# Modulation of a two-layer diffusion trunk: its products between the large ones in bursts of eight row blocks instead of four

## The chip, the cores and the metric

One core of a Trainium2 chip runs the whole program. The metric is device time in microseconds (us) of one execution, the median of several. TensorE multiplies, VectorE and ScalarE do the elementwise work, GpSimd a little of it, and SyncE issues nearly all DMA transfers, in one queue.

## The reference

One inference step of a trunk of two layers, for 128 context tokens and 128 latent tokens with the same weights, all in float32. For each layer:

```
mod = SiLU(cond) @ w_mod[l] + b_mod[l]      # cond: 2 vectors of 2048; w_mod[l]: 2048 x 12288
sh1, sc1, g1, sh2, sc2, g2 = split(mod, 6)
h   = rmsnorm(x) * (1 + sc1) + sh1
mix = mixers(h @ w_in)                      # latent attention | 2-D Fourier | RWKV-7 scan
x   = x + g1 * rmsnorm(mix @ w_out)
h   = rmsnorm(x) * (1 + sc2) + sh2
u   = dwconv3(h @ w_up) + b;  gate, val = split(u, 2)
x   = x + g2 * rmsnorm((silu(gate) * val) @ w_down)
```

The modulation is a product of two rows with 100 MB of weights per layer. Its first part is needed before the first product of a layer, its last part at the end.

## The kernel before

**Large products.** The 256 tokens (both groups side by side) are the moving operand, 128x128 pieces of a weight are the stationary one. To keep float32 accuracy each operand is split in two float32r halves: `hi` is the rounded value, `lo` the rest. `mm3` (lines 335 to 339) multiplies hi by hi, hi by lo and lo by hi: three products on TensorE for each piece. For the weights `weights_` (line 312) loads a tile of 128x2x512 into one of the 7 buffers of the pool `raw` (512 KB), ScalarE writes `hi` (L327), VectorE writes `lo` (L328). Pools of 3 hold the hi and the lo. A weight's instructions are traced 60 places ahead of their turn (`WP`), so that it is loaded and split early. For the input h of a sub-layer `pre_norm` (line 465) makes, for each of four groups of 512 features, eight pieces `h` on VectorE (L485), eight `hh` on ScalarE (L486) and eight `hl` on VectorE (L487).

**Modulation.** `modulation` (line 232) makes 512 of the 12288 columns. The stationary operand is a 128x32 piece of the silu of the two conditions (2 of 32 columns are used), the moving one a row block of 128 rows by 512 columns of w_mod. The 16 row blocks are spread over four strips of 32 columns of the array (q), so that four products can run at the same time; each strip sums every fourth block in its own 32 partitions of the PSUM tile `mb`. Then VectorE transposes `mb` to `pm` (L245), TensorE adds up the four strips (`mc`, L249), VectorE adds the bias (`mod`, L254) and makes scale factors of it (`modx`, L288 and L290). Being float32, each of these products stands as two records in the trace.

**How it is spread.** `modulation` is a generator. A step (`mod_step`, line 258) is one advance of it: four row blocks (two loads of 512 KB with two row blocks each, then the four products), or the transpose. 48 such generators stand in a queue in a fixed order. `gemm` and `gemm_k` call `tick` after each half tile of weights; `tick` (line 275) adds a rate, set by hand for each stage (`MR`, `AR`, `QR`, `FR`), to a credit, and makes a step for each full credit. `need` makes steps until a given group is done; `pre_norm` and the last parts of each sub-layer call it. Before the first layer's mixers (`early`) the modulation's rows lie in the pool of slabs (20 buffers), later in the pool `raw`, which they share with the weights.

**Order.** The program is traced by one Python process; a scheduler then orders each engine's instructions by priority (the place at which they were traced, moved by `WP` for the weights) and by when it reckons that their inputs and buffers are there. On the chip every engine and SyncE's queue go through their list in that order.

Of the kernel before, what the change touches and what calls it, by code (L numbers as in the profile page):

```python
# [38 lines left out]
NV, NV2 = sum(r for _, r in VEC), sum(r for _, r in VEC2)  # L39


# buffers of each pool; columns of the modulation made before the first layer; pieces that GpSimd takes; order of the pieces
RAW, HI, SLAB, HALF = 7, 3, 20, 22
BMM = 3
SV = 4
# [1 line left out]
POOLX = (5, 6)  # L47
ORD = (0, 1, 5, 2, 3, 6, 4, 7)
YG = ((0, 1), (5,), (2, 3), (6,), (4,), (7,))
# how the steps of the scan and of the modulation are spread over the products, by layer and phase  # L50
RA = [
    [[0.8, 0.8, 0.8], [0.8, 1.16, 0.96], [0.56, 0.8, 0.8], [0.8], [0.95, 0.95, 0.95, 0.95], [0.95, 1.0, 0.8, 1.0], [1.0, 1.0, 1.3]],
    [[0.8, 0.8, 0.578], [0.88, 0.8, 0.8], [0.96, 0.8, 0.8], [1.0], [1.0, 1.0, 1.0, 1.0], [1.287, 1.3, 1.183, 1.3], [1.45, 1.45, 1.45]],
# [15 lines left out]


class Lazy:
    """the items of a generator, traced as they are asked for"""

    def __init__(self, gen):
        self.gen, self.items = gen, []
# [7 lines left out]
class Trunk:  # L83
# [47 lines left out]
        o = VOFF[name] + k0  # L131
        return (self.vec2 if name.startswith("ffn") else self.vec[l])[:, o:o + n]

    # ---------------------------------------------------------------- set-up
    def setup(self):
        nc, i = self.nc, self.i
        self.const = self.cp.tile([128, C_LATER], F32, name="const")
        nc.sync.dma_start(self.const, i["const"][:, 0:C_LATER])
        self.later = self.cp.tile([128, C_N - C_LATER], F32, name="later")
        self.ident = self.c(C_ID, 128)  # L140
        self.eps = self.cp.tile([128, 2], F32, name="eps")
        nc.vector.memset(self.eps[:, 0:1], EPS)
        nc.vector.memset(self.eps[:, 1:2], GN_EPS)
        self.zero = self.cp.tile([128, 64], F32, name="zero")
        nc.vector.memset(self.zero, 0.0)
        self.seg = self.cp.tile([128, 256], F32, name="seg")
        nc.vector.memset(self.seg, 1.0)
        nc.vector.memset(self.seg.rearrange("p (s t) -> p s t", t=128)[:, :, 0:1], 0.0)
        self.vec = [self.cp.tile([128, NV], F32, name=f"vec{l}") for l in range(L)]
        self.mod = [self.cp.tile([128, 96, 2], F32, name=f"mod{l}") for l in range(L)]  # L150
        self.modx = [self.cp.tile([128, 4, 16, 2], F32, name=f"modx{l}") for l in range(L)]

        cr = self.small([32, 128], "vr", bufs=1)
        nc.sync.dma_start(cr[0:16], i["c_ctx"].rearrange("(k p) -> k p", p=128))
        nc.sync.dma_start(cr[16:32], i["c"].rearrange("o (k p) -> (o k) p", p=128))
        self.cst = self.cp.tile([128, 16, 32], F32, name="cst")
        nc.vector.memset(self.cst, 0.0)
        b = self.bank([128, 2, 16])
        nc.tensor.transpose(b.rearrange("p g k -> p (g k)"), cr, self.ident[0:32, 0:32])
        nc.scalar.activation(self.cst[:, :, 0:2], b.rearrange("p g k -> p k g"), AF.Silu)  # L160

        self.new_x()
        for g, nm in enumerate(("x_prompt", "x_sample")):
            for k in range(4):
                if k % 2 == 0:
                    r = self.raw([128, 8, 128])
                    nc.sync.dma_start(r, i[nm][0, :, 512 * k:512 * k + 1024].rearrange("t (k p) -> t k p", p=128))
                b = self.bank([128, 4, 128])
                for j in range(4):
                    nc.tensor.transpose(b[:, j, :], r[:, 4 * (k % 2) + j, :], self.ident)  # L170
                for e in range(2):
                    nc.vector.tensor_copy(self.x[2 * k + e][:, :, 128 * g:128 * g + 128], b[:, 2 * e:2 * e + 2, :])

        for _ in range(SV):
            self.mod_step()
        self.finish(self.load_vec(0, VEC, self.vec[0]))

    def new_x(self):
# [51 lines left out]
        return r  # L230

    def modulation(self, l, i):
        """512 columns of the modulation on the tensor engine: every fourth chunk of the rows in a strip of 32 columns"""
        nc = self.nc
        w = self.i["w_mod"][l]
        b = self.pmod.tile([128, 512], F32, tag="m", name=self.name("mb"))
        for kg in range(4):
            for e in range(2):
                r = self.mod_raw(w, i, 512 * kg + 256 * e)
                for f in range(2):  # L240
                    q = 2 * e + f
                    nc.tensor.matmul(b[32 * q:32 * q + 32, :], self.cst[:, 4 * kg + q, :], r[:, f, :], start=kg == 0, stop=kg == 3)  # L242
            yield
        m = self.half([128, 4, 4, 32], nm="pm")
        nc.vector.transpose(m.rearrange("p j a c -> p (j a c)"), b)  # L245
        yield
        b2 = self.pmod.tile([128, 4, 2], F32, tag="m", name=self.name("mc"))
        for a in range(4):
            nc.tensor.matmul(b2[32 * a:32 * a + 32], self.c(C_SEL, 32), m[:, :, a, 0:2], start=True, stop=True)  # L249
        self.mod_end(l, i, b2)  # L250
# [7 lines left out]
    def mod_step(self):  # L258
        while True:
            if self.modgen is None:  # L260
                if not self.modq:
                    return False
                self.modgen = self.modulation(*self.modq[0])
            try:
                next(self.modgen)
                return True
            except StopIteration:
                self.modgen = None
                self.done.add(self.modq.pop(0))
# [5 lines left out]
    def tick(self, n=1.0):  # L275
        self.credit += self.rate * n
        while self.credit >= 1:
            self.credit -= 1
            self.mod_step()

    def mod_scale(self, l, which, k):
        nc = self.nc
# [6 lines left out]
        else:  # L289
            nc.vector.tensor_tensor(out, src, g, op=ALU.mult)  # L290

    # ---------------------------------------------------------------- pieces
    def split(self, src, nm):
        nc = self.nc
        hi = self.slab(list(src.shape), F32R, nm + "h")
# [70 lines left out]
                    self.tick(0.5)  # L366

    def gemm_k(self, wsrc, cols, rhs, evac, rates):
        """like gemm, one group of 512 input features after the other, with all the sums open at once"""
        banks = []  # L370
        for c0, w in cols:
            banks.append([(self.mm_bank if n < BMM else self.bank)([128, 2, 256])
# [47 lines left out]
            nc.tensor.matmul(ps, self.c(C_ONE, 128), sq[:, j, :], start=first and j == 0, stop=last and j == n - 1)  # L420

    def sumsq4(self, ps, src, c0):
        """like sumsq over 16 chunks, with the sums of every fourth chunk in a strip of 32 columns"""
        nc = self.nc
        n = src.shape[1]
        sq = self.half([128, n, 256], nm="sq")
        nc.scalar.activation(sq, src, AF.Square)
        for j in range(n):
            c = c0 + j
            q = 32 * (c % 4)  # L430
            nc.tensor.matmul(ps[q:q + 32, :], self.c(C_ONE, 32), sq[:, j, :], start=c < 4, stop=c >= 12)  # L431
# [7 lines left out]
        return out  # L439

    def rsqrt(self, out, src, scale, eps, tmp):
        """out = 1 / sqrt(scale * src + eps): the table's value, then a Newton step"""
        nc = self.nc
        v, t = tmp
        nc.scalar.activation(out, src, AF.Abs_reciprocal_sqrt, bias=self.eps[:, eps:eps + 1], scale=scale)
        nc.scalar.activation(v, src, AF.Identity, bias=self.eps[:, eps:eps + 1], scale=scale)
        nc.vector.scalar_tensor_tensor(t, out, -0.5, out, op0=ALU.mult, op1=ALU.mult)
        nc.vector.tensor_tensor(t, t, v, op=ALU.mult)
        nc.vector.scalar_tensor_tensor(out, t, 1.5, out, op0=ALU.add, op1=ALU.mult)  # L449
# [5 lines left out]
        return rs  # L455

    def arm(self, after):
        """brings in the table that the next norm needs, once after is there"""
        t = self.small([128, 2], "arm", bufs=1)
        self.nc.scalar.activation(t, after, AF.Abs_reciprocal_sqrt, bias=self.c(C_ONE, 1), scale=0.0)  # L460

# [1 line left out]
        return rs.unsqueeze(1).to_broadcast([128, n, 256])  # L463

    def pre_norm(self, l, which):
        """a generator: the normed and modulated input, split, by groups of 512 features"""
        nc = self.nc
        sh0 = (0, 48)[which]
        a = self.modx[l][:, 2 * which]
# [43 lines left out]
            nc.vector.scalar_tensor_tensor(uv[:, :, 1:128], pv[:, :, 0:127], w0, uv[:, :, 1:128], op0=ALU.mult, op1=ALU.add)  # L513
            nc.vector.scalar_tensor_tensor(uv[:, :, 0:127], pv[:, :, 1:128], w2, uv[:, :, 0:127], op0=ALU.mult, op1=ALU.add)  # L514

    # ---------------------------------------------------------------- mixers
    def in_proj(self, l, h, st, names, outer=False):
        nc = self.nc
        cols = {"kv": (512, 320), "q": (0, 512), "xf": (832, 512), "r": (1344, 512), "k": (1856, 512), "v": (2368, 512), "lo": (2880, 256)}
# [187 lines left out]
    def rwkv_scan(self, l, st):  # L707
# [16 lines left out]
        U = {}  # L724

        def pre(z):
            """normalised key, token-major values (as they are and reversed) of two channel chunks"""
            kh = self.half([128, 2, 256], nm="kh")
            tt(kh, st["k", z], b2(vec("rwkv_k_k", 2 * z, 2), 256), op=ALU.mult)
            wa = self.half([128, 2, 256], nm="wa")  # L730
# [204 lines left out]
    def rwkv_solve(self, l, st, z):  # L935
# [6 lines left out]
        C = st["C"][z]  # L942
        AP, RH, bon, lo = C["AP"], C["RH"], C["bon"], st["lo"]
        y, v = st["rw", z], st["v", z]
        # inverses of the 32 x 32 blocks on the diagonal
        G = self.slab([128, 32, 32], nm="G")
        nc.gpsimd.memset(G[:, :, 16:32], 0.0)
        for d in range(2):
# [18 lines left out]
                yield INV * IW  # L967
        XT = M
        nc.vector.transpose(XT.rearrange("p n t -> p t n"), X)
        # solve block by block; the right-hand side turns into the solution  # L970
        for j in range(4):
            js = slice(32 * j, 32 * j + 32)
            for d in range(2):
# [26 lines left out]
                           start=d == 0 and e == 0 and g == 0, stop=d == 1 and g == 1 and e == 1)  # L1000
        tt(y, y, ya.rearrange("p e g t -> p e (g t)"), op=ALU.add)
        yield YW
        # group norm, bonus, gate
        sv = self.half([128, 2, 256], nm="sq")
        g2 = self.half([128, 256], nm="g2")
        nc.sync.dma_start(g2, i["rwkv_g2"][l][:, 256 * z:256 * z + 256])
# [51 lines left out]
            nc.gpsimd.dma_start(o["state"][0, l, d, 4 * z:4 * z + 4].rearrange("h v k -> v h k"), so.rearrange("v (h k) -> v h k", k=64))  # L1058
            yield TW

    # ---------------------------------------------------------------- layer
    def merge(self, a, b, na, nb):
        """a's steps with b's spread over them"""
        credit = 0.0
        for _ in a:
            credit += nb / na
# [205 lines left out]
```

## Time and profile before

| | |
|---|---|
| time, median of 3 runs | 2782.31 us (2780.23 to 2782.39) |
| profiled execution, first to last instruction | 2799.7 us |
| instructions | 53893 |
| TensorE busy | 2701.2 us, 96% |
| VectorE, ScalarE, GpSimd busy | 61%, 43%, 4% |
| moved by DMA | 594 MB, 212 GB/s on average |
| granted clock of TensorE, mean | 0.979 |

The profile is one execution, not one of the three timed ones; the page gives no other time of it than its span. Stages of the span, roughly: up to 165 us set-up and the first layer's first in_proj (k, r, v and the low-rank columns); to 600 us its mixers with the rest of in_proj and the output projection; to 1490 us its gated MLP; to 2020 us the second layer's in_proj and mixers; then the second layer's MLP. The modulation is spread from 13 to 1890 us.

In a row of the timeline the columns are start, duration, engine, line, operation, output and inputs, shapes and count; in brackets stands the idle time ahead of it and what ended that. In a table of windows: stretch, its length, busy time of TensorE with the number of its records, granted clock (1.00 is 2.4 GHz, 0.50 is 1.2), busy share of the DMA engines and GB/s.

### The profile page before, as it was taken

The numbers are of one execution on the slowest core, as the hardware profiler recorded it, in microseconds if no ns is written. First come the engines' busy times: TensorE is split into PE (matmuls) and PEld (weight loads), VectorE is DVE, ScalarE is ACT, GpSimd is POOL, SyncE is SP. The second block draws the span as 40 slices with busy tenths as digits, with TensorE's granted clock in tenths as the row PEclk, the third lists the DMA queues.
The fourth block names the chain that finished last, engine by engine and source line by source line (L and its number), as shares of the span: only waits on it lengthen the run. The fifth ranks groups of instructions, "written<-read, shape, count | busy, mean of one in ns | idle before, by whom it ended". The sixth has DMA issues, their size and how long they took to land. (4 is left out here: it accounts for less than half of the span.)

```text
span 2799.7 us, 53893 instructions
## 1 busy us (share of the span) xinstructions
PE 2701.2 (96%) x22531; PEld 2383.4 (85%) x22531; DVE 1695.1 (61%) x2690; ACT 1208.4 (43%) x1747; POOL 124.8 (4%) x130
## 2 busy tenths in 40 slices
PE   7999999989999999999998999999799999999997
PEld 4577778758888988888886987878699999999997
DVE  3377848576564465545556688685766546654665
ACT  2256424344343344334444466353454434443453
POOL 1111000010000000000000020000100000000000
PEclk9999989999999999999999999998899999999998
DMA  9965636778777877788776654443355555555552
GB/s 364 372 208 179 204 102 209 239 249 273 262 260 266 273 265 264 263 268 271 250 256 203 215 184 152 162 141 132 97 181 181 184 185 181 182 183 186 181 181 84
DMA packets 316501, 594.46 MB, mean 212 GB/s; under 512 B 22758, under 2 KB 38146, under 8 KB 316256
## 3 DMA queue, kind: packets, MB, share of 16 engines
q1 hardware_dynamic: 314624, 589.54, 63.5%
q8 instruction: 177, 2.90, 0.4%
q0 software_dynamic: 1632, 1.46, 0.2%
q14 instruction: 68, 0.56, 0.1%
HBM read 583.78 MB, written 7.14 MB: 211 GB/s over the span
## 5 line engine op out<-in xcount | busy, mean ns | idle before, releaser
L328 DVE TENSOR_TENSOR lo<-raw,hi 128x1024 fp32r<-128x1024 f32 (+1 forms) x712 | 854.8, 1204 | 756.0 <-ACT hi L327 716.1
L327 ACT CAST hi<-raw 128x1024 fp32r<-128x1024 f32 (+1 forms) x712 | 733.0, 1030 | 1035.1 <-PE mm L338 839.0
L337 PE MATMUL mm<-hh,hi 128*128 128x256 f32 x3360 | 958.9, 288 | 9.6 <-ACT hh L486 8.7
L338 PE MATMUL mm<-hl,hi 128*128 128x256 f32 x3360 | 953.1, 284 | 1.5 <-DVE hl L487 0.8
L339 PE MATMUL mm<-hh,lo 128*128 128x256 f32 x3360 | 950.7, 284 | 0.9 <-DVE lo L328 0.9
L337 PEld LDWEIGHTS mm<-hh,hi 128*128 128x128 f32 x3360 | 644.4, 192 | 79.4 <-issue 57.9
L338 PEld LDWEIGHTS mm<-hl,hi 128*128 128x128 f32 x3360 | 646.5, 192 | 10.1 <-issue 6.0
L339 PEld LDWEIGHTS mm<-hh,lo 128*128 128x128 f32 x3360 | 645.9, 192 | 5.7 <-issue 3.5
L337 PE MATMUL mm<-gh,hi 128*128 128x256 f32 x1408 | 401.2, 286 | 0.0
L339 PE MATMUL mm<-gh,lo 128*128 128x256 f32 x1408 | 398.8, 283 | 0.0
L338 PE MATMUL mm<-gl,hi 128*128 128x256 f32 x1408 | 398.5, 283 | 0.0
L337 PEld LDWEIGHTS mm<-gh,hi 128*128 128x128 f32 x1408 | 269.6, 192 | 22.8 <-issue 22.6
L339 PEld LDWEIGHTS mm<-gh,lo 128*128 128x128 f32 x1408 | 269.9, 192 | 4.1 <-issue 4.1
L338 PEld LDWEIGHTS mm<-gl,hi 128*128 128x128 f32 x1408 | 270.0, 192 | 3.3 <-issue 3.3
L242 PE MATMUL mb<-raw,cst 128*32 128x512 f32 x1536 | 256.3, 612 | 8.3 <-DMA raw<-in_w_mod 4.3
L510 ACT ACTIVATE u<-mm,vec 128x256 f32<-128x256 f32 x176 | 94.6, 562 | 115.8 <-DVE u L514 84.1
L337 PE MATMUL mm<-mxh,hi 128*128 128x256 f32 x384 | 117.2, 307 | 0.3 <-ACT hi L327 0.3
L338 PE MATMUL mm<-mxl,hi 128*128 128x256 f32 x384 | 112.3, 293 | 0.3 <-DVE mxl L298 0.3
L339 PE MATMUL mm<-mxh,lo 128*128 128x256 f32 x384 | 111.5, 292 | 0.6 <-DVE lo L328 0.6
L513 DVE SCALAR_TENSOR_TENSOR u<-mm,vec,u 128x254 f32<-128x254 f32 x176 | 80.1, 475 | 32.7 <-ACT u L510 32.7
L337 PEld LDWEIGHTS mm<-mxh,hi 128*128 128x128 f32 x384 | 75.3, 197 | 21.0 <-issue 16.6
L496 POOL TENSOR_TENSOR d<-d,rs 128x512 f32<-128x512 f32 x8 | 13.4, 1694 | 1713.0 <-DVE rs L449 1713.0
(344 smaller groups left out, 3130.0 us busy)
## 6 DMA issues: line engine op xcount, KB each, us to landing
raw<-in_w_mod SPq DMA_DIRECT2D x384, 512.0 KB, 5.5
raw<-in_ffn_w_up SPq DMA_DIRECT2D x352, 512.0 KB, 4.5
raw<-in_ffn_w_down SPq DMA_DIRECT2D x176, 512.0 KB, 4.7
raw<-in_w_in SPq DMA_DIRECT2D x80, 512.0 KB, 5.2
raw<-in_w_out SPq DMA_DIRECT2D x64, 512.0 KB, 5.4
raw<-in_w_uq SPq DMA_DIRECT2D x16, 384.0 KB, 4.9
raw<-in_w_in SPq DMA_DIRECT2D x16, 320.0 KB, 3.3
raw<-in_w_in SPq DMA_DIRECT2D x16, 256.0 KB, 3.7
```

What stands on the lines that cost most here:

```text
L242: nc.tensor.matmul(b[32 * q:32 * q + 32, :], self.cst[:, 4 * kg + q, :], r[:, f, :], start=kg == 0, stop=kg == 3)
L327: nc.scalar.copy(hi[:, :, 0:w], r)
L328: nc.vector.tensor_tensor(lo[:, :, 0:w], r, hi[:, :, 0:w], op=ALU.subtract)
L337: mm(out, whi, xhi, start=start, stop=False)
L338: mm(out, whi, xlo, start=False, stop=False)
L339: mm(out, wlo, xhi, start=False, stop=stop)
L496: e.tensor_tensor(d, d, self.bc(rs, 2), op=ALU.mult)
L510: nc.scalar.activation(u[:, m, :], ps[:, m, :], AF.Identity, scale=w1, **kw)
L513: nc.vector.scalar_tensor_tensor(uv[:, :, 1:128], pv[:, :, 0:127], w0, uv[:, :, 1:128], op0=ALU.mult, op1=ALU.add)
```

## The change

A burst takes eight row blocks: `modulation` now asks for four loads at once (four tiles of 512 KB) and then traces eight products, two for each strip, before it yields. `mod_step` returns how many of the old steps that was (2 for a burst, 1 for the transpose), and `tick` takes it from the credit, so that the average rate is as before. Lines behind the change move by one, and comments are gone; both are left out here.

```
-        for _ in range(SV):
-            self.mod_step()
+        n = 0
+        while n < SV:
+            n += self.mod_step()
...
-        for kg in range(4):
-            for e in range(2):
-                r = self.mod_raw(w, i, 512 * kg + 256 * e)
-                for f in range(2):
-                    q = 2 * e + f
-                    nc.tensor.matmul(b[32 * q:32 * q + 32, :], self.cst[:, 4 * kg + q, :], r[:, f, :], start=kg == 0, stop=kg == 3)
-            yield
+        for k2 in range(0, 4, 2):
+            rs = [self.mod_raw(w, i, 512 * k2 + 256 * e) for e in range(4)]
+            for kg in (k2, k2 + 1):
+                for q in range(4):
+                    r = rs[2 * (kg - k2) + q // 2]
+                    nc.tensor.matmul(b[32 * q:32 * q + 32, :], self.cst[:, 4 * kg + q, :], r[:, q % 2, :], start=kg == 0, stop=kg == 3)
+            yield 2
         m = self.half([128, 4, 4, 32], nm="pm")
         nc.vector.transpose(m.rearrange("p j a c -> p (j a c)"), b)
-        yield
+        yield 1
...
                 if not self.modq:
-                    return False
+                    return 1
                 self.modgen = self.modulation(*self.modq[0])
             try:
-                next(self.modgen)
-                return True
+                return next(self.modgen)
...
         while self.credit >= 1:
-            self.credit -= 1
-            self.mod_step()
+            self.credit -= self.mod_step()
```

Three places show what this does to the order. Names: `mb` is the sum of one modulation group, `raw` a loaded tile, `gh` and `gl` the halves of the MLP's inner values, `hi` and `lo` those of a weight; a number counts tiles and differs between the two programs.

On TensorE, in the first layer's MLP (its first down-projection), before: two bursts of four, 48 large products apart.

```order
4919 L339 MATMUL mm_8970<-gh_8695,lo_9172 128x256
4920 L242 MATMUL mb_9100<-raw_9205,cst 32x512 x2
4921 L242 MATMUL mb_9100<-raw_9209,cst 32x512 x2
4922 L337 MATMUL mm_8969<-gh_8695,hi_9177 128x256
...
4969 L339 MATMUL mm_9242<-gh_6964,lo_9246 128x256
4970 L242 MATMUL mb_9100<-raw_9279,cst 32x512 x2
4971 L242 MATMUL mb_9100<-raw_9283,cst 32x512 x2
4972 L337 MATMUL mm_9241<-gh_6964,hi_9251 128x256
```

The same place now:

```order
4919 L338 MATMUL mm_8972<-gh_8703,lo_9180 128x256
4920 L243 MATMUL mb_9040<-raw_9213,cst 32x512 x2
4921 L243 MATMUL mb_9040<-raw_9215,cst 32x512 x2
4922 L243 MATMUL mb_9040<-raw_9217,cst 32x512 x2
4923 L243 MATMUL mb_9040<-raw_9219,cst 32x512 x2
4924 L336 MATMUL mm_8971<-gh_8703,hi_9185 128x256
```

The second burst of four has moved up to the first; the next burst of eight stands 175 large products further on.

On VectorE, in the first layer's first in_proj, where the second group of 512 features begins, before (`x` is the residual stream, `rs` its norm factor):

```order
55 L328 TENSOR_TENSOR lo_708<-raw_705,hi_707 128x1024
56 L328 TENSOR_TENSOR lo_714<-raw_711,hi_713 128x1024
57 L245 STREAM_TRANSPOSE pm_659<-mb_566 128x512
58 L254 TENSOR_TENSOR mod_100<-mc_661,vec_98 128x8
59 L288 SCALAR_TENSOR_TENSOR modx_102<-mod_100,vec_98 128x8
60 L485 SCALAR_TENSOR_TENSOR h_679<-x_114,modx_102,rs_284 128x128 x3
61 L487 SCALAR_TENSOR_TENSOR hl_678<-h_679,mod_100,hh_677 128x128
62 L485 SCALAR_TENSOR_TENSOR h_679<-x_114,modx_102,rs_284 128x128
63 L487 SCALAR_TENSOR_TENSOR hl_678<-h_679,mod_100,hh_677 128x128 x3
64 L485 SCALAR_TENSOR_TENSOR h_692<-x_115,modx_102,rs_284 128x128 x3
```

Now:

```order
50 L246 STREAM_TRANSPOSE pm_659<-mb_530 128x512
51 L255 TENSOR_TENSOR mod_100<-mc_661,vec_98 128x8
52 L287 SCALAR_TENSOR_TENSOR modx_102<-mod_100,vec_98 128x8
53 L484 SCALAR_TENSOR_TENSOR h_687<-x_114,modx_102,rs_284 128x128 x4
54 L484 SCALAR_TENSOR_TENSOR h_700<-x_115,modx_102,rs_284 128x128
55 L327 TENSOR_TENSOR lo_716<-raw_713,hi_715 128x1024
56 L484 SCALAR_TENSOR_TENSOR h_700<-x_115,modx_102,rs_284 128x128 x2
57 L327 TENSOR_TENSOR lo_722<-raw_719,hi_721 128x1024
58 L484 SCALAR_TENSOR_TENSOR h_700<-x_115,modx_102,rs_284 128x128
59 L486 SCALAR_TENSOR_TENSOR hl_686<-h_687,mod_100,hh_685 128x128 x4
60 L486 SCALAR_TENSOR_TENSOR hl_686<-h_700,mod_100,hh_685 128x128 x4
```

The two lo have moved from ahead of the transpose to between the h, and all hl behind the last h. The third and the fourth group read alike; at the first all eight h stand ahead of the hl, without a lo among them.

In SyncE's queue, in the MLP, before:

```order
410 L317 DMA raw_8761<-in_ffn_w_down 128x2x512
411 L317 DMA raw_8767<-in_ffn_w_down 128x2x512
412 L229 DMA raw_8797<-in_w_mod 128x2x512
413 L229 DMA raw_8801<-in_w_mod 128x2x512
414 L317 DMA raw_8829<-in_ffn_w_down 128x2x512
```

Now:

```order
412 L316 DMA raw_8769<-in_ffn_w_down 128x2x512
413 L316 DMA raw_8775<-in_ffn_w_down 128x2x512
414 L230 DMA raw_8805<-in_w_mod 128x2x512
415 L230 DMA raw_8807<-in_w_mod 128x2x512
416 L230 DMA raw_8809<-in_w_mod 128x2x512
417 L230 DMA raw_8811<-in_w_mod 128x2x512
418 L316 DMA raw_8845<-in_ffn_w_down 128x2x512
```

Four loads of modulation stand in a row where there were two.

## Rows read from the trace of the kernel before

**Rows 1.** Head of the page: span, TensorE and VectorE (busy, share, instructions).

```profile
span 2799.7 us, 53893 instructions
PE 2701.2 (96%) x22531; PEld 2383.4 (85%) x22531; DVE 1695.1 (61%) x2690; ACT 1208.4 (43%) x1747; POOL 124.8 (4%) x130
```

**Rows 2.** Table of windows, TensorE, one window for each stage.

```profile
13.00:165.00 152.00, 140.15 (x938) 0.99 0.91 329
165.00:600.00 435.00, 412.86 (x3721) 0.97 0.62 207
600.00:1490.00 890.00, 886.22 (x7257) 1.00 0.78 261
1490.00:2020.00 530.00, 491.79 (x4279) 0.94 0.49 157
```

**Rows 3.** Timeline of TensorE: a burst of four in the first MLP.

```profile
999.20 0.28 PE L339 MATMUL mm<-hh,lo 128*128 128x256 f32 x1
999.41 1.07 PE L242 MATMUL mb<-raw,cst 128*32 128x512 f32 x8
...
1000.63 0.28 PE L338 MATMUL mm<-hl,hi 128*128 128x256 f32 x1
```

**Rows 4.** Timeline of TensorE: a burst of eight in the first mixer stage.

```profile
495.46 0.28 PE L339 MATMUL mm<-mxh,lo 128*128 128x256 f32 x1
495.67 1.92 PE L242 MATMUL mb<-raw,cst 128*32 128x512 f32 x14
...
497.74 0.28 PE L338 MATMUL mm<-mxl,hi 128*128 128x256 f32 x1
```

**Rows 5.** Timeline of TensorE: second group of the first in_proj begins.

```profile
77.22 0.25 PE L249 MATMUL mc<-pm,const 128*32 128x8 f32 x8 [0.86 <-DVE pm L245]
77.75 1.05 PE L242 MATMUL mb<-raw,cst 128*32 128x512 f32 x4 [0.29 <-DVE mod L254]
79.06 0.51 PE L337 MATMUL mm<-hh,hi 128*128 128x256 f32 x2 [0.26 <-ACT hh L486]
79.69 0.38 PE L338 MATMUL mm<-hl,hi 128*128 128x256 f32 x1
```

**Rows 6.** Timeline of VectorE at the same place.

```profile
77.93 0.88 DVE L485 SCALAR_TENSOR_TENSOR h<-x,modx,rs 128x128 f32<-128x128 f32 x3
78.75 0.35 DVE L487 SCALAR_TENSOR_TENSOR hl<-h,mod,hh 128x128 fp32r<-128x128 f32 x1
...
82.44 1.23 DVE L328 TENSOR_TENSOR lo<-raw,hi 128x1024 fp32r<-128x1024 f32 x1 [0.38 <-ACT hi L327]
```

**Rows 7.** Table of windows, TensorE: behind two such groups, and in layer two.

```profile
80.00:83.40 3.40, 3.40 (x12) 0.50 1.05 387
119.00:123.50 4.50, 4.19 (x32) 1.00 1.04 385
...
1517.60:1523.70 6.10, 6.09 (x28) 0.50 0.14 53
```

**Rows 8.** Timeline of TensorE: first large product of layer two.

```profile
1517.61 1.01 PE L337 MATMUL mm<-hh,hi 128*128 128x256 f32 x3 [3.21 <-ACT hh L486]
```

**Rows 9.** Page, DMA issues: count, KB each, median us from issue to landing.

```profile
raw<-in_w_mod SPq DMA_DIRECT2D x384, 512.0 KB, 5.5
raw<-in_ffn_w_up SPq DMA_DIRECT2D x352, 512.0 KB, 4.5
...
raw<-in_x_sample SPq DMA_DIRECT2D x2, 512.0 KB, 7.4
```

**Rows 10.** Groups by line, 600 to 1490 us: busy us, mean ns, idle before.

```profile
L328 DVE TENSOR_TENSOR lo<-raw,hi 128x1024 fp32r<-128x1024 f32 x262 | 319.9, 1222 | 343.0 <-ACT hi L327 306.3 <-PE mb L242 36.3
L327 ACT CAST hi<-raw 128x1024 fp32r<-128x1024 f32 x262 | 274.1, 1046 | 451.2 <-PE mm L338 408.9 <-DMA raw<-in_ffn_w_up 19.1 <-issue 12.1
```

## What I expected

> **What bounds the kernel now.** I read the head of the page first: TensorE is busy for 2701.2 of 2799.7 us, VectorE for 61% of them [rows 1]. The page gives this execution no other time than its span; it lies 17.4 us above the median of the timed runs, so I sum against the span and take the difference off the median of 2782.3.
>
> Then I cut the span into stages [rows 2]. The reader is to see that they differ. From 600 to 1490 us, the first layer's gated MLP, TensorE has 3.8 us of 890 free: whatever it is spared there comes off the time. In the two mixer stages (165 to 600, and 1490 to 2020) it is busy for 95% and 93%. In the first 152 us it is busy for 92% while the transfers run at 329 GB/s; there the modulation of this very layer is awaited, group by group.
>
> Last I looked at single bursts in the timeline of TensorE. A burst of four (eight records, since each of these products leaves two) starts 0.21 us after the product before it, where neighbours among the large products stand 0.12 apart, and the second product behind it starts 1.43 us after the one ahead of it [rows 3]: less two ordinary steps the burst costs 1.19 us. A burst of eight stands once in the trace with large products on both sides: 2.28 us less 0.24, or 2.04 [rows 4] (14 of its 16 records are there). Four products run side by side, one in each strip, so a burst of eight is two rounds. One round is therefore 2.04 - 1.19 = 0.85 us, and 1.19 - 0.85 = 0.34 us is what one switch from full-width products to strips and back costs.
>
> **The change, part by part.** No product and no transfer is added or taken away. What changes is how many bursts there are, and the order.
>
> *Fewer switches.* In the order of TensorE I counted uninterrupted runs of modulation products: 217 before, 152 now; rounds: 233 and 230. By stage:
> - The first layer's MLP: 92 runs with 93 rounds become 45 with 89 (four bursts had been cut in one and three, and such a piece costs a whole round). 47 x 0.34 + 4 x 0.85 = 19.4 us, all of it where TensorE has no gap.
> - The first mixer stage: 52 with 58 become 38 with 57: 14 x 0.34 + 0.85 = 5.6 us. Some of it falls where TensorE waits for the scan anyway; I take 4.5 (bounds 2 and 5.6).
> - From the end of that MLP on: 28 with 30 become 20 with 31: 8 x 0.34 - 0.85 = 1.9 us; I take 1.2 (bounds 0 and 1.9).
> - The first in_proj: 45 with 52 become 49 with 53. Here the two products of one transfer still stand alone between the large ones, as before; nothing is merged, and 4 x 0.34 + 0.85 = 2.2 us are lost.
>
> *A new wait in the first in_proj.* This is what the diff doesn't show. At each of its four groups of 512 features the chain is: last burst, transpose, mc, mod, modx, h, hh, hl, first large product. Before, VectorE makes three h, then the first hl, and the low halves of the weights (lo) come ahead of the chain or after it. Now, at three of the four groups, it makes five h, a lo, two h, a lo, one h, and only then the first hl, while TensorE's second large product wants two of them. From the trace: h to h is 0.27 us, an hl ends 0.35 after it starts, a lo of 128x1024 takes 1.23 [rows 6]. Counted from the first h, the second hl ends at 5 x 0.27 + 1.23 + 2 x 0.27 + 1.23 + 0.27 + 0.27 + 0.35 = 5.2 us. Before, the first product that wants hl started at 79.69, 1.76 us after the first h at 77.93 [rows 5, 6], and TensorE had by then idled some 0.5 us behind its burst. Now it has a burst (1.0 us) and one product to do until about 1.4 us and then waits to 5.3: 3.9 us idle, 3.4 more than before. Three times 3.4 is 10.2 us. Queued behind the hl on VectorE is the next pair of lo, which TensorE wants some 50 products later, so nothing more grows from it. At the first group all eight h come before the hl but no lo: 0.5 us. Bounds for the four together: 3 us (if TensorE arrives late for other reasons) and 13 us.
>
> *The clock.* The stretch after the second of these groups ran at a granted clock of 0.50, that is 1.2 GHz, for 3.4 us, which costs 1.7; the other two, of the same make, kept 2.4 GHz (the one at 119 is shown, that at 156.5 reads alike) [rows 7]. Ahead of each TensorE had stood still in three waits of at most 0.86 us [rows 5]. Where it had idled 3.21 us ahead of the first product of a group, in layer two, the clock was 0.50 for 6.1 us [rows 7, 8]. With 3.9 us of idling I take the fall at all three: two more at 1.7, 3.4 us; bounds 0 and 3 x 3.05 - 1.7 = 7.5.
>
> The Trainium skill (TensorE: Matmul & The Clock Gate, section HAM oscillation) says that a wait between bursts of matmuls puts the array back to half rate so that the work behind each wait starts cold, every time. By that rule all three groups fall, as I have taken it; by the rows before, where one in three fell, the term would be near nothing and the time 3 us lower.
>
> *The order elsewhere.* On VectorE and TensorE the scan and the heads move by some ten places against the large products in both mixer stages. No row prices that; I take 0, within 5 us either way.
>
> Sum: 19.4 + 4.5 + 1.2 - 2.2 - 10.2 - 0.5 - 3.4 = 8.8 us less. 2799.7 becomes 2790.9, and the median 2782.3 becomes 2773.5; I forecast 2774.
>
> **The transfers.** Four of the seven raw buffers now hold modulation at once, which leaves three to the weights. A weight tile holds its buffer from issue to its lo: 4.5 us to land [rows 9], 1.05 for hi and 1.22 for lo [rows 10], 6.8 together. Three buffers give a tile each 2.3 us; TensorE uses one in 24 x 0.12 = 2.9. And up to three tiles are already split ahead. So I cost it at nothing; the cover is gone where landing takes over 3 x 2.88 - 2.27 = 6.4 us.
>
> **Rivals.**
> - *The new wait hides.* If TensorE is late at those three groups in any case, or the second hl is not what it waits for, neither the 10.2 nor the 3.4 is paid (3 remain): 2774 - 11 = 2763. For it: the first stage is also the one where transfers run fullest. Against: with the DMA engines that full TensorE still had waits under 0.9 us at the group [rows 5], so data is there.
> - *The clock takes the rest.* If each of the three waits halves the clock for 6.1 us as in layer two, 7.5 are paid for 3.4, and if the mixer stages give their lower bounds (2 and 0), 3.7 more are gone: 2774 + 4 + 4 = 2782, no change.
> - *The weights starve (slower).* In the MLP, 262 weight tiles of 128x1024 are split [rows 10], about half of them while a burst holds four buffers. It decides from a landing of 6.4 us. The fastest kinds land in 4.5, the modulation itself in 5.5, the input x_sample, 512 KB as well, in 7.4 [rows 9]. At 7.4 each such tile would come (7.4 + 2.27) / 3 - 2.88 = 0.34 us late: 131 x 0.34 = 45 us, and the time 2774 + 45 = 2819. For it: four transfers of 512 KB now stand in one row of the queue. Against: the median of those weights, and the three tiles split ahead.
> - *The change does not merge.* So it is in the first in_proj; elsewhere the order shows bursts of eight in 65 places or so, and order is fixed when the program is built. No chance of its own.
>
> **How the numbers follow.** Forecast 0.50, hidden wait 0.22, clock 0.18, starving 0.10. The forecast's own range is 2766 to 2781: the bounds of the mixers, of the clock and of the order elsewhere, not all at one end. The range is 2759 to 2787: it takes in the hidden wait and the clock, and leaves out the starving and some tails. What a measurement of this kernel tells from no change is about 0.2%, 5.6 us: faster is below 2776.7, slower above 2787.9. Faster: 0.7 of the forecast, nearly all of the hidden wait and a little of the clock, 0.59. Same: the rest of the forecast and most of the clock, 0.29. Slower: 0.12.
>
> **What would show it.** Right: between 600 and 1490 us runs of sixteen records at 0.21 + 1.85 us, and that stage some 19 us shorter, with no wait for a weight transfer; in the first 165 us three gaps of 3 to 4 us on TensorE ahead of an hl product, released by L486 (hl, L487 before), with clock 0.50 behind them, and that stage longer by 12 to 17 us. Wrong: a gap at those groups below 1 us; a clock of 0.50 within the MLP; lo or hi of the MLP waiting for raw with TensorE idle behind it; or the mixer stages changed by over 6 us.

## The result: slower by 0.8%

The changed kernel takes 2812.01 us (median of 6 runs, 2804.88 to 2814.47), the kernel before beside it 2782.62 (6 runs, 2780.23 to 2803.16). The ratio is 1.0079, with a 95% interval of 1.0052 to 1.0105. Forecast were 2774 us and, with 0.59, a faster kernel. The prediction was wrong, in sign as well.

The profiled execution of the changed kernel is its fastest run. Head of its page, for [rows 1], and two of its DMA issues, for [rows 9]:

```profile
span 2803.1 us, 53919 instructions
PE 2682.2 (96%) x22531; PEld 2383.6 (85%) x22531; DVE 1698.8 (61%) x2690; ACT 1207.0 (43%) x1747; POOL 108.9 (4%) x130
...
raw<-in_w_mod SPq DMA_DIRECT2D x384, 512.0 KB, 6.9
raw<-in_ffn_w_up SPq DMA_DIRECT2D x352, 512.0 KB, 4.4
```

TensorE is busy for 19 us less than in [rows 1], and yet the span is longer: what is saved is lost elsewhere, and more. (A second profile of the kernel before, below, has 2684.8 us of busy time: most of these 19 us are not the change's.) The modulation's transfers land 1.4 us later than before, the MLP's weights no later.

A burst of eight in the first MLP, timeline of TensorE, for [rows 3, 4]:

```profile
1001.35 0.28 PE L338 MATMUL mm<-hh,lo 128*128 128x256 f32 x1
1001.55 1.92 PE L243 MATMUL mb<-raw,cst 128*32 128x512 f32 x16
```

Start of the second group of the first in_proj, TensorE, for [rows 5]:

```profile
79.60 0.25 PE L250 MATMUL mc<-pm,const 128*32 128x8 f32 x8 [0.87 <-DVE pm L246]
80.14 1.06 PE L243 MATMUL mb<-raw,cst 128*32 128x512 f32 x8 [0.29 <-DVE mod L255]
81.45 0.38 PE L336 MATMUL mm<-hh,hi 128*128 128x256 f32 x1 [0.25 <-ACT hh L485]
85.36 0.58 PE L337 MATMUL mm<-hl,hi 128*128 128x256 f32 x1 [3.53 <-DVE hl L486]
```

VectorE at that place, for [rows 6]:

```profile
80.32 1.40 DVE L484 SCALAR_TENSOR_TENSOR h<-x,modx,rs 128x128 f32<-128x128 f32 x5
81.64 1.22 DVE L327 TENSOR_TENSOR lo<-raw,hi 128x1024 fp32r<-128x1024 f32 x1
82.77 0.61 DVE L484 SCALAR_TENSOR_TENSOR h<-x,modx,rs 128x128 f32<-128x128 f32 x2
83.30 1.22 DVE L327 TENSOR_TENSOR lo<-raw,hi 128x1024 fp32r<-128x1024 f32 x1
84.43 0.35 DVE L484 SCALAR_TENSOR_TENSOR h<-x,modx,rs 128x128 f32<-128x128 f32 x1
84.69 2.19 DVE L486 SCALAR_TENSOR_TENSOR hl<-h,mod,hh 128x128 fp32r<-128x128 f32 x8
```

Five h, a lo, two h, a lo, one h, and then the hl: TensorE has nothing to do for 3.53 us. The table of windows behind the three group starts, for [rows 7], shows what follows each:

```profile
83.50:90.30 6.80, 4.94 (x14) 0.50 1.06 379
127.90:134.70 6.80, 4.81 (x14) 0.50 0.90 286
172.30:179.10 6.80, 4.78 (x14) 0.50 0.44 107
```

6.8 us at 1.2 GHz each time, where before one of the three starts had 3.4. The Trainium skill (TensorE: Matmul & The Clock Gate, section HAM oscillation) says that a wait between bursts of matmuls puts the array back to half rate and that the work behind it starts cold, and the trace agrees at all three groups. Each fall begins some 2 us before the wait ends, and that part costs nothing:

```profile
83.50:85.36 1.86, 0.00 (x0) 0.52 1.05 387
```

What a fall costs is therefore counted from the busy time in it, half of which is an estimate of the loss: (4.94 + 4.81 + 4.78) / 2 = 7.3 us for the three.

**Where the time went.** The two profiles at hand differ by 3.4 us only, the medians by 29: the first profile of the kernel before was a long execution. So I took a second one (first experiment, span 2784.2). Cutting both kernels at the same large products makes the stages comparable: set-up, first in_proj, first layer's mixers, first MLP, second layer's in_proj and mixers, second MLP. The first cut, near 64 us, lies among bursts and is some nine products apart in the two, so set-up and first in_proj are best taken together. Table of windows, TensorE (columns as in [rows 2]), second profile of the kernel before:

```profile
4.20:64.80 60.60, 49.76 (x297) 0.97 1.04 379
64.80:173.50 108.70, 104.15 (x731) 0.98 0.84 299
173.50:613.40 439.90, 414.83 (x3761) 0.98 0.62 205
613.40:1518.30 904.90, 891.58 (x7280) 0.99 0.78 261
1518.30:1959.50 441.20, 431.00 (x3979) 0.99 0.52 167
1959.50:2777.00 817.50, 792.19 (x6491) 0.98 0.53 167
```

The changed kernel:

```profile
4.40:63.20 58.80, 47.02 (x296) 0.97 1.04 381
63.20:193.50 130.30, 115.54 (x738) 0.92 0.76 266
193.50:635.90 442.40, 413.85 (x3754) 0.97 0.60 200
635.90:1522.30 886.40, 875.51 (x7288) 0.99 0.78 268
1522.30:1979.60 457.30, 437.37 (x3969) 0.97 0.49 159
1979.60:2797.00 817.40, 792.10 (x6491) 0.98 0.52 168
```

Length less busy time is idle time; half of the busy time at 0.50 is the estimate of what the clock cost. Set-up and first in_proj: +19.8 us (189.1 against 169.3), of it 11 idle (26.5 against 15.4), 5.7 clock (7.3 against 1.6) and 2.0 for six more runs of bursts at 0.34. First mixers: +2.5; by itself that shows nothing, since eight profiles with bursts of four in this stage lie between 439.7 and 449.2 us. MLP: -18.5. Second layer's in_proj and mixers: +16.1, of it 9.7 idle (19.9 against 10.2) and 10.5 clock (12.7 against 2.2), less 4.1 for twelve runs of bursts fewer (15 against 27). Two falls make the 12.7:

```profile
1722.00:1728.80 6.80, 4.97 (x29) 0.50 0.02 4
1909.70:1930.20 20.50, 20.50 (x146) 0.50 0.10 33
```

The two spans differ by 19 of the 29 us between the medians. The other five runs of the changed kernel lie 6 to 10 us above the profiled one; where they lose that, no trace shows. The experiments ask where the differences come from.

### The profile page after: what moved, and what is told of

Same layout as the page of the kernel before. It is cut to its first block, busy times and chain, and to the rows that moved or that the text cites. A ratio compares the mean times of both kernels' runs of the same rounds, so it can differ in the third digit from the quotient of the medians.

```text
span 2803.1 us, 53919 instructions
## 1 busy us (share of the span) xinstructions
PE 2682.2 (96%) x22531; PEld 2383.6 (85%) x22531; DVE 1698.8 (61%) x2690; ACT 1207.0 (43%) x1747; POOL 108.9 (4%) x130
## 5 line engine op out<-in xcount | busy, mean ns | idle before, releaser
L243 PE MATMUL mb<-raw,cst 128*32 128x512 f32 x1536 | 243.3, 613 | 11.3 <-DMA raw<-in_w_mod 7.8
L243 PEld LDWEIGHTS mb<-raw,cst 128*32 128x32 f32 x1536 | 46.2, 110 | 88.8 <-issue 48.7
```

## Experiments

All use one kernel in which the size of a burst goes by the stage of the program. Stage 0 is set-up and first in_proj, 1 the first layer's mixers, 2 its MLP, 3 the second layer's first in_proj, 4 its mixers, 5 its MLP, where no modulation is left. With no stage listed every engine has the order of the kernel before, with all listed the source makes that of the changed one. Lines are those of this kernel; the comments in the cuts from it are added here.

```
+            if self.stage in BIG and k2 % 2 == 0:   # four loads, eight products, yield 2
...
+            else:                                   # two loads, four products, yield 1
```

**The kernel before once more** (`BIG = ()`).

> The kernel before, unchanged in every engine's order (bursts of four everywhere), for a second profile of it. The two profiles so far differ by 3.4 us of span, the medians by 29, so some 18 us that the first profiled execution of the kernel before lost are not in its other runs. If the profile of before was an odd execution: time 2780 to 2784, span near 2780, with the low-clock stretches at 363, 589, 1899 and 1985 us shorter or gone. If every profiled execution is longer: time 2782 in the timed runs, span again near 2799.

2783.71 us (12 runs), ratio 0.9993 (0.9971 to 1.0015). The first profile was an odd execution. Cut at the same products, its second layer:

```profile
1522.50:1974.70 452.20, 441.70 (x3978) 0.97 0.51 163
...
1899.40:1926.60 27.20, 27.20 (x196) 0.50 0.14 45
```

27.2 us at 0.50 near 1900 us, against none there in the second profile, and the stage is 11.0 us longer (452.2 against 441.2). In the first mixers it has a fall of 17.1 us at 363, where the second has 3.4, and that stage is 5.8 us longer (445.7 against 439.9). These two make up the 15.5 us between the spans, less shorter falls that only the second has. Of 29 other runs of the kernel before, 8 took over 2794 us.

**Eight from the first mixers on** (`BIG = (1, 2, 3, 4, 5)`).

> Bursts of four through set-up and the first in_proj (as before), bursts of eight from the first mixers on. Theory (the loss is the wait for hl and the clock behind it at the three group starts of the first in_proj, about 22 us; the first MLP gains 19): the order of VectorE at the three starts is that of before again, time 2758 to 2770. Rival (the loss is spread over the mixers of both layers or comes with the bursts of eight as such, and the 22 us between the two profiles at the end of the first in_proj belong to one execution): time 2785 to 2812.

2790.54 us (12 runs; eight of them 2789.6 to 2792.3, the fastest 2775.5), ratio 1.0016 (1.0002 to 1.0030). The time is the rival's, and half of each reason: the loss of the first in_proj is gone (107.3 us), the MLP has its gain (886.3), and yet nothing is won over the kernel before. The second layer takes 463.3 us. So the first in_proj is one cause of two.

**Eight up to the first in_proj only** (`BIG = (0,)`).

> The other half: bursts of eight only in set-up and the first in_proj, bursts of four from the first mixers on. Theory: three gaps of 3.5 us on TensorE ahead of hl and granted clock 0.50 for 6.8 us behind each; time 22 us above before, 2800 to 2810. Rival (loss elsewhere): 2778 to 2790.

2808.97 us (6 runs), ratio 1.0089 (1.0070 to 1.0108): the first cause by itself. The stage takes 130.4 us, the second layer 440.1, with the wait and the clock as expected (second group; the other two alike):

```profile
85.63 0.58 PE L350 MATMUL mm<-hl,hi 128*128 128x256 f32 x1 [3.52 <-DVE hl L499]
```

**Eight in the MLP only** (`BIG = (2,)`).

> Bursts of eight only in the first layer's MLP, four everywhere else. Theory: 47 runs fewer at 0.34 us and four rounds at 0.85, so 19 us less than before: 2760 to 2767, and the mixers of both layers as before. Rival (a longer MLP gain is given back by a clock that falls later, or by late weights): 2772 to 2785.

2780.20 us (12 runs), ratio 0.9976 (0.9956 to 0.9995): the rival's time, for neither's reason. The MLP takes 889.2 us, 15.7 less than before. But the second layer, in fours again, takes 448.5 instead of 441.2 (in this profile the first mixers, in fours too, are 9.3 us longer as well, with 37.5 us at 0.50):

```profile
1509.00:1957.50 448.50, 433.90 (x3970) 0.99 0.51 162
```

Its order is not that of before: while the program is traced, the modulation stands one step further at the end of the MLP, with the same credit. The step comes from `need`. A group counts as done only when the next step is asked for, and that step is the next group's first burst. It is made outside the credit, and it has eight row blocks now. So the average rate is not as before, as the section on the change says; at the end of the MLP the trace has 1368 records of the modulation instead of 1360 (1370 in the changed kernel).

**The two lo behind the hl** (all stages).

```
-                wt = self.weights(wsrc[...], 4, w)
+                wt = self.ahead(20 if self.early else WP, self.weights_, wsrc[...], 4, w)
```

> Bursts of eight everywhere, as in the changed kernel; only in the first in_proj of both layers' common helper, while the first layer's runs, a weight's instructions are traced 20 places ahead instead of 60. On VectorE the two lo of 1.22 us then stand behind the eight hl at the group starts instead of between the h. Theory A (the order of VectorE is what TensorE waits for, and the clock falls behind a long wait): the three waits for hl shrink from 3.5 to about 1.1 us, the granted clock stays at 1.00 behind them; first in_proj 7 + 10 us shorter than in the changed kernel's profile (130.3 us between the same two products), time 2793 to 2800. Rival B (the waits shrink but the clock falls at a group start anyway): 7 us, time 2803 to 2807. Rival C (the two lo are then late themselves, for the hh x lo products): time 2810 or more.

2797.42 us (6 runs), ratio 1.0051 (1.0036 to 1.0066): 14.6 us below the changed kernel. The time is theory A's, the reason only half. At the three starts the product of hh now waits 2.08 us for hi, and that of lo 0.44 to 0.92 us; at the second group:

```profile
80.77 0.58 PE L349 MATMUL mm<-hh,hi 128*128 128x256 f32 x1 [2.08 <-ACT hi L339]
82.44 0.58 PE L351 MATMUL mm<-hh,lo 128*128 128x256 f32 x1 [0.44 <-DVE lo L340]
```

Together they are some 2.5 to 3 us in two waits instead of 3.5 in one, and the clock still falls at two of the three (6.8 and 3.4 us). Set-up and first in_proj take 173.5 us instead of 189.1. Of these 15.6 us the idle time gives 5.0 (21.5 against 26.5), the clock some 2.5, and the bursts, which stand in 41 runs instead of 53, some 4; the rest I can't place.

**Extra products in the wait** (all stages).

```
+                                if fill:   # 8 in the first in_proj behind the first group's start, else 0
+                                    self.nc.tensor.matmul(p[:, m, :], hi[:, kk, s], xh[:, 2 * k2 + kk, :], start=False, stop=False)
+                                    for _ in range(fill):
+                                        self.nc.tensor.matmul(p[0:64, m, :], self.zero, self.c(C_ID, 256), start=False, stop=False)
...
```

> The changed kernel with eight extra products on TensorE (a stationary of zeros, 64 columns, moving 128x256, float32, added to the open sum, so that they change no value) behind the first hh product of the second, third and fourth group of the first in_proj. They stand in the time in which TensorE waits for hl. Theory (the fall of the clock behind the wait is a price of its own, 6.8 us at 0.50 and so 3.4 us each): the hl products start when they did, the clock stays at 1.00 behind them, the stage is 8 to 10 us shorter than in the changed kernel, time 2801 to 2805. Rival (the clock is low there for another reason, or the extra products only add to the path): same as the changed kernel or up to 4 us slower, 2810 to 2816.

2800.29 us (6 runs), ratio 1.0059 (1.0042 to 1.0076): 11.7 us below the changed kernel, with more work. VectorE still makes the hl last. Table of windows, TensorE, from each of the three starts on:

```profile
82.00:98.00 16.00, 16.00 (x108) 1.00 1.06 383
126.00:142.00 16.00, 16.00 (x128) 1.00 1.01 368
170.00:186.00 16.00, 16.00 (x136) 1.00 0.74 240
```

No idle time and a full clock: the fall goes with the wait ahead of it and is a price of its own. The fill is not clean. The extra products take 4.1 us at each start, more than the wait that they fill, a burst of eight moved in as well, and the product of hl starts 6.2 us behind that of hh instead of 3.9. The first in_proj, cut at the same products:

```profile
63.60:180.20 116.60, 113.97 (x786) 1.00 0.84 297
```

It is 13.7 us shorter than in the changed kernel, more than the 8 to 10 expected. The 12 us of idle time that are gone went into 12 us of extra products; of the gain the clock gives 7.3 and seven runs of bursts fewer (31 against 38) 2.4, and the rest I can't place. In this profile the second layer is 11.0 us longer than in the changed kernel's (468.3 against 457.3), with 47.8 us at 0.50.

**Fours in the second layer, credit realigned** (`BIG = (0, 1, 2)`).

```
+                if gg == 10:             # last piece of the MLP
+                    self.stage = 9       # in no list: bursts of four
+                    self.credit -= 1
```

> Bursts of eight up to the last piece of the first layer's MLP, bursts of four from there on; one credit is taken back at that point, so that from the second layer on every engine has the order of the kernel before. Between the same two products the second layer's in_proj and mixers take 441.1 us in a typical profile of before and 457.2 in the changed kernel (idle 10.2 against 19.9, clock 2.2 against 13.7 us lost). Theory (merging there makes new waits, and with them a fall of the clock at about 1900 us): that stage is back at 438 to 441 us where the clock does not fall, 452 where it does as in before's first profile; time 14 us below the changed kernel, 2794 to 2801. Rival (the loss there belongs to single executions): 2808 to 2814.

2791.05 us (12 runs), ratio 1.0025 (1.0008 to 1.0041); the second layer takes 440.1 us, with a clock of 1.00. The second cause lies there, and it is worth 21 us of the median, more than the 14 that I expected.

**Eight in the MLP, credit realigned** (`BIG = (2,)`, the same three lines).

> Bursts of eight only in the first layer's MLP up to its last piece, four elsewhere, with the credit taken back as in the run above, so that the second layer's order is that of before (in the earlier run with eight in the MLP alone each call that finishes a group overshot by eight row blocks instead of four, and the second layer ran one step ahead: 8 us lost there). Theory: the MLP's 16 to 18 us are kept, time 2763 to 2769, with single executions 14 us above where the clock falls at 1900 us. Rival (the second layer loses what the MLP gains in any order): 2776 to 2783.

2769.62 us (6 runs), ratio 0.9948 (0.9934 to 0.9962): faster than both kernels, if by 0.5% only. The second layer takes 440.1 us. This run and the last changed two things at once, the size of the bursts in the second layer and the credit. The next two and the last two tell them apart.

**Eight in one part of the second layer** (`BIG = (2, 3)`, then `(2, 4)`, with the credit).

> The best version so far (bursts of eight in the first layer's MLP up to its last piece, 2769.6 us), and eight also in the second layer's first in_proj; its mixers in fours. Theory (the loss of the second layer comes with its mixers, where TensorE waits for the scan's VectorE work, and the in_proj only trades some 1.5 us of switches for as much waiting for lo): the second layer's stage between the same two products 439 to 444 us against 440.1, time 2768 to 2773. Rival (the waits for lo at the in_proj are where the loss begins, and the clock at 1900 us follows): stage 448 or more, time 2778 to 2790.

> The best version so far and eight also in the second layer's mixers, behind its first in_proj, which is in fours. Theory: idle time of that stage up from 10.9 to 16 us or more, and the granted clock falls to 0.50 near 1890 us in nearly every execution; stage 450 to 460 us, time 2780 to 2790. Rival (the in_proj is the cause): stage 436 to 442, time 2765 to 2770.

2771.55 us (7 runs), ratio 0.9950 (0.9928 to 0.9973), stage 439.5 us; and 2774.08 us (12 runs), ratio 0.9959 (0.9944 to 0.9973), stage 440.4. My theory for the second of these fell. Eight in the mixers adds 3.4 us of idle time (14.3 against 10.9) and saves about as much (eight runs of bursts fewer); no fall of the clock near 1900 us, and no 450 us.

**Eight in the first layer's mixers too** (`BIG = (1, 2)`, with the credit).

> The best version so far and eight also in the first layer's mixers. The prediction counted 52 runs of bursts that become 38 and 4.5 us for it. Theory (the runs go, and as much idle time comes, 28.5 us in the changed kernel against 25.1): stage within 2 us of 430 apart from the clock, time 2767 to 2773. Rival (as predicted): 2764 to 2766. Rival (more falls of the clock): 2775 or more.

2769.39 us (12 runs), ratio 0.9950 (0.9931 to 0.9969): no gain from it. Ten runs of bursts fewer at 0.34 us are 3.4 us, and the stage's idle time is up from 24.6 to 28.7 us. So it is in all profiles: 22.4 to 25.6 us of idle time in this stage with bursts of four, 28.3 to 32.5 with eight.

**Eight to the end of the MLP** (`BIG = (2,)`, `self.credit -= 1` alone).

> Bursts of eight through the whole MLP of the first layer, its last piece too, with the one credit taken back; four elsewhere. The last piece has some 5 more pairs to merge at 0.34 us: 1 to 2 us below the best version so far, 2767 to 2769. Rival (the second layer's first in_proj no longer has quite the order of before, and that costs more than it brings): 2771 or more.

2771.21 us (11 runs), ratio 0.9950 (0.9931 to 0.9969): no difference that could be told.

**The changed kernel with the credit alone, and that without the first in_proj** (`BIG = (0, 1, 2, 3, 4, 5)`, then `(1, 2, 3, 4, 5)`).

```
+                if gg == 10:
+                    self.credit -= 1
```

> The changed kernel, bursts of eight everywhere, with one line more: one credit is taken back in the last piece of the first layer's MLP, which undoes the step that the bursts of eight run ahead (each call that finishes a group goes on to the next group's first burst, and that has eight row blocks now). On TensorE the last modulation products then stand 25 rows of the program from where they stood before, instead of 154 earlier. Theory (the second layer's loss is this shift, not the size of the bursts): the second layer's stage 438 to 446 us against 457.2 in the changed kernel, no low clock near 1900 us, time 2793 to 2801. Rival (eight in both parts of the second layer loses although each part alone does not): 452 to 462 us, time 2806 to 2814.

> As the run above, and bursts of four up to the end of the first in_proj: the change without the waits for hl and without the shift. Theory: 2764 to 2771 us, the 19 us of the MLP with nothing given back. Rival (the shift is not the second cause): 2785 to 2791, as in the run with eight from the first mixers on.

2792.14 us (12 runs), ratio 1.0019 (1.0002 to 1.0035): one line, which changes only when the bursts come, takes 20 us off the changed kernel. And 2769.70 us (7 runs), ratio 0.9934 (0.9909 to 0.9958): the change without its two accidents is 0.7% faster than the kernel before (whose runs beside it have a median of 2786.29; against the 2783 to 2784 of its earlier runs it is 0.5%). The fifth row of the windows of these two:

```profile
1528.40:1969.30 440.90, 427.08 (x3979) 1.00 0.52 168
```
```profile
1503.30:1944.20 440.90, 426.67 (x3977) 1.00 0.52 168
```

Bursts of eight through the whole second layer, and no loss. With the earlier runs this makes all four cases of that stage: in fours 441.2 us without the shift and 448.5 with it, in eights 440.9 without it and 457.3 (463.3 in the second experiment) with it. The size of the bursts alone costs nothing there, the shift alone 7 us, and both together 16 and more.

The shift is visible where the modulation ends. Last modulation products and first step of the scan's last solve (px), TensorE, in the kernel before (second profile):

```profile
1886.32 1.06 PE L255 MATMUL mb<-raw,cst 128*32 128x512 f32 x6
...
1894.22 0.96 PE L1001 MATMUL px<-rh,M 32*32 32x64 f32 x14 [0.50 <-DVE M L981]
```

In the changed kernel:

```profile
1874.03 1.05 PE L243 MATMUL mb<-raw,cst 128*32 128x512 f32 x2
...
1907.48 1.91 PE L988 MATMUL px<-rh,M 32*32 32x64 f32 x31 [0.48 <-DVE modx L289]
```

With the credit:

```profile
1891.98 1.92 PE L247 MATMUL mb<-raw,cst 128*32 128x512 f32 x16
...
1901.06 1.13 PE L1001 MATMUL px<-rh,M 32*32 32x64 f32 x17 [0.33 <-DVE M L981]
```

The modulation was through 33 us ahead of px instead of 8 (9 with the credit). Earlier in the stage other products wait longer than before; the two longest waits:

```profile
1619.94 0.38 PE L338 MATMUL mm<-hh,lo 128*128 128x256 f32 x1 [1.52 <-DVE lo L327]
...
1723.22 0.44 PE L870 MATMUL b<-kr,zero 64*64 64x128 f32 x1 [2.77 <-DVE s L842]
```

At the place of the second, a burst stood some 1 us ahead before, and the wait was 0.57 us (second profile):

```profile
1711.59 1.07 PE L255 MATMUL mb<-raw,cst 128*32 128x512 f32 x8
...
1714.93 0.29 PE L883 MATMUL b<-kr,zero 64*64 64x128 f32 x1 [0.57 <-DVE s L855]
```

In the changed kernel no burst stands there, and the fall at 1722 us begins within the wait. That the missing burst makes the wait longer I read from this one place; no run tests it by itself. With the credit the stage's idle time is 13.8 us, 3.6 above that of before, so not all of the idle time is the shift's.

## Why the prediction was wrong

- *Fewer switches, MLP: right.* 19.4 us were predicted, 18.5 are measured (904.9 to 886.4), at 0.20 + 1.86 us a burst. The nearness is in part luck: between these cuts 44 runs of bursts fewer (52 against 96) are 15.0 us, and 2.4 are idle time (13.3 to 10.9), of which I had counted none. Later experiments kept the gain: 887.0 in the last one.
- *The new wait in the first in_proj: right.* Three waits of 3.53 us at the place and from the order named (3.9 minus the 0.5 of before were counted). At the first group TensorE waited 1.1 us for hl where 0.5 were counted. Idle time up to the end of the first in_proj grew by 11 us, where 10.7 were predicted.
- *The clock: the mechanism right, the size too small but within its bounds.* Counted were two more falls of 1.7 us, 3.4 with 7.5 as the upper bound; measured 5.7. I took the busy time in a fall from the one that followed three short waits, 3.4 us. Behind a wait of 3.5 us it is 4.8 to 4.9, towards the 6.1 of layer two [rows 7], which I had kept for a bound. With the lost switches (2.2 predicted; six more runs, 2.0) set-up and first in_proj cost 19.8 instead of 16.3 us; 1 us of that I can't place.
- *First mixers: the 4.5 us that I counted as gained did not come.* The switches are saved and as much idle time comes; the eleventh experiment shows it alone.
- *The step that failed: "The order elsewhere", taken as 0 within 5 us, and with it the 1.2 us gained from the end of the MLP on.* It was 16.1 us lost in the second layer in these profiles, 20 in the medians (2812.01 against 2792.14 with one credit taken back). I had counted runs and rounds by stage, and what they save there is right (4.1 us for twelve runs fewer); what also moved was their place against the large products. I took the rate as equal to that of before, though `need` makes a burst outside the credit, and so one step of four row blocks more stood ahead of the second layer. Of the some 28 us between the forecast's sum and these profiles this step is 17, the first mixers are 4.5 to 7, set-up and first in_proj 3.5, the MLP 1.
- *The rivals.* Starving weights did not happen: the MLP's transfers land in 4.4 us, below the 6.4 from which that decided. The hidden wait was wrong as well. The rival on the clock named the right mechanism for the first in_proj; its price of 7.5 us lies above the measured 5.7, the forecast's 3.4 below. None named the second layer.
- *What would show it* listed "the mixer stages changed by over 6 us" as a sign of error, and this is the one that came. Of the signs of being right, the MLP's and the three gaps came too; the first stage was to be 12 to 17 us longer and was 19.8.

What stays open is why the shift makes the clock fall near 1900 us. In the four profiles with eight shifted (changed kernel, second, fifth and sixth experiment) it fell there, for 20.5 to 27.3 us. In the other profiles it did so once in twelve, in the first profile of the kernel before. The fourth experiment has the shift in fours and no fall there. That taking the shift away takes most of the added idle time and this fall away is shown, in one profile of each kernel; what sets the fall off there is not, and the first profile of before shows that it needs no shift.

## What to carry to other kernels

Work that is dropped between other work at a rate is not moved by its average alone: follow where each unit lands, and what calls make steps outside the credit, before a change in its size is priced. A wait of some 3.5 us ahead of a dense stretch costs it twice, here 3.5 us in idle time and some 2.4 in clock behind it, so order on the engine that feeds TensorE, or other work put in the gap, is worth more than the gap. Before two profiles are compared, see that each one's time is near its kernel's median, and cut both at the same products.

## What the runs showed that I had not expected

- At twelve of twelve waits of 3.5 us (three in each of four kernels) the clock fell to 0.50 for 6.8 us, from before the end of the wait on; at three starts with two waits of 2.1 and 0.4 to 0.9 us it fell at two, for 6.8 and 3.4 us, and not at one of those with 0.9.
- The same order on every engine ran with and without 27.3 us at 0.50 near 1900 us, in two profiles of 2799.7 and 2784.2 us.
- The modulation's median landing time grew from 5.5 to 6.9 us when four loads stood in a row, and no large product of the MLP waited for it.
